# Value products of two attention units issued together, with six transposed blocks in flight

## The chip, the cores and the metric

One core of one Trainium2 chip runs the whole program. The metric is the device time of one execution in microseconds, as the median of several runs. The engines are named as the profile names them: PE is TensorE (PEld its weight loads), DVE is VectorE, ACT is ScalarE, POOL is GpSimd, and SP is SyncE, which here only issues DMAs.

## The reference, cut to what matters

One step of a hybrid layer: 2048 latent tokens on a 32 x 64 grid and 128 context tokens share one input projection of width 3840. Three branches read it: a gated short convolution, a chunked spatial gate and an attention over 8 heads of 64. The change touches the first and the last.

```
ya  = ba * conv3(ca * xa) * silu(ga)                # depthwise, over tokens, 256 channels
s   = q k_window * scale + bias[window], masked     # 8 x 16 window of the grid
s_c = q k_context * scale                           # 128 cached context keys
p   = softmax([s, s_c])
yc  = (p_window v_window + p_context v_context) * silu(gc)
out = concat(ya, yb, yc) @ w_out                    # then residual and LayerNorm
```

## The kernel before, in words

Each float32 operand is split into a high and a low float16 half, and a product is three matmuls (high x high, high x low, low x high). The order of instructions on every engine is the order in which the program emits them. The program keeps a planner's clock `now` in nanoseconds: each projection matmul of n columns advances it by n/2.4 (`tick`), and every event that is due is emitted there. `post(delay, f)` sets an event, `drain(tags)` emits events of a kind at once.

After the first stage (normalisation, spatial gate, values) the kernel runs projection jobs, each over five token tiles (four of 512, one of 128). Per pair of heads `hp` (0 to 3) they are q, k, gc and then some of xa, ca and the double job ba/ga (after hp 1 and hp 3). After each k job an `Attn` object posts 17 units of attention (16 blocks of 128 grid queries, and the context queries as unit 16), so that attention of `hp` runs inside the projections that follow it.

A unit `u` has two heads `h`. `scores(u, h)` issues four matmuls into the PSUM tile `s` and the sum with bias and maximum on DVE (L1041, into `pt`). Then, by `a_step` after it: `expo` (ACT, L1050), `norm` (DVE), `high` (ACT, L1057, the high half of the probabilities into `PH`), `low` (DVE, L1060, the low half, and then POOL's table of bias and mask for three half units later, L998 and L1002), and `turn` (a DMA transpose on SP, L1067, from `PH` into `ptr`). `a_val` after the second head's `turn`, `values` issues the value products into the PSUM tile `o` (L1086: 6 matmuls of 64 columns per chunk of 128 keys, 4 or 5 chunks, one chunk for unit 16), and DVE gates the result (L1094, L1101). Half units follow each other at half of `pace`.

The double job ba/ga has two projections a tile, here called P1(t) and P2(t), t = 0 to 4. The convolution of tile t, conv(t), is five POOL instructions (L1181, L1184) into the tile `cvt`. DVE multiplies P1 into it (L1194); ACT takes the tanh of P2 (L553), DVE makes the gate (L554) and the product ya(t) (L1199), and SP stores it (L1200). All projections share three PSUM buffers (`PJ = 3`), so P2(4) takes the buffer of P1(3), which L1194 of tile 3 frees.

Near the end of the last double job `open_out` loads `w_out` in eight blocks through three buffers (`wos`, L1139); `wo_split(k)` splits each on ACT (L1144) and DVE (L1145), and a block's load can be issued when the split three before it is done. `first_out` loads the first rows of the concatenated branches, and `out_split` splits them (L1127, L1128). Then the output projection runs (L1333).

Of the kernel before, what the change touches and what calls it, by code (L numbers as in the profile page):

```python
# [22 lines left out]
P = 128  # L23
D = 1024
KB = 8
LAT = 2048
# [65 lines left out]
    a_val=(5700.0, 7500.0, 6200.0, 5600.0),  # L92
    a_step=(700.0, 700.0, 2100.0, 2750.0, 3700.0),
    out_open=1000.0,
# [44 lines left out]
def hybrid_step(ctx: ExitStack, tc: tile.TileContext, x_prompt, x_sample, cache_k, cache_v, c, c_ctx,  # L139
# [56 lines left out]
    ones = cons.tile([P, P], F32, name="ones")  # L196
    G.memset(ones, 1.0)

# [50 lines left out]
    xg, xp = open_pool("xphase", side="right")  # L249
    mg, modp = open_pool("modp", side="left")  # L250
# [88 lines left out]
    wsp = tmpA.tile([P, 4, P], F32, name="wsp", tag="cvt", bufs=2)  # L339
# [358 lines left out]
    def load_cache():  # L698
# [3 lines left out]
        ck_sb = tmpA.tile([P, 512], F32, name="ck_sb", tag="cvt", bufs=2)  # L702
# [302 lines left out]
    class Attn:  # L1005
        def __init__(self, hp, pace):
            self.hp = hp
            self.ys = None
            self.ts = {}
            for u in range(17):  # L1010
                for h in range(2):
                    post(T['a_start'][hp] + (u + T['a_half'] * h) * pace, lambda u=u, h=h: self.scores(u, h), ("as", hp, u))

        def scores(self, u, h):
# [24 lines left out]
            pt = ap.tile([P, 608], F32, name="pt", bufs=3)  # L1039
# [24 lines left out]
            def turn():  # L1064
                drain(("av", self.hp, u - T['av_guard']))
                t = ap.tile([P, 10, P], F16, name="ptr", bufs=4)
                SP.dma_start_transpose(out=t[:, 0:2 * wp // P, :], in_=pb[:, 0:2 * wp])  # L1067
                self.ts[u, h] = t
                if h == 1:
                    post(T['a_val'][self.hp], lambda: self.values(u, [self.ts.pop((u, e)) for e in range(2)], wp // P, n), ("av", self.hp, u))  # L1070
# [4 lines left out]
        def values(self, u, t, nch, n):  # L1075
            hp = self.hp
            o = aps.tile([P, P], F32, name="o", tag="o")
            for ch in range(nch):
                if ch == 0:
                    vt, kk = (v_ctx if u < 16 else v_pr)[:, hp, :], P  # L1080
                else:
                    rb, j = UNITS[u]
                    vt, kk = VW[:, RB_ROW0[rb] // 4 + ch - 1, j, :], min(P, n - (ch - 1) * P)
                for i, (a, b) in enumerate(((0, 0), (0, 1), (1, 0))):
                    for h in range(2):
                        PE.matmul(out=o[64 * h:64 * h + 64, :], lhsT=vt[0:kk, a * P + 64 * h:a * P + 64 * h + 64],  # L1086
                                  rhs=t[h][0:kk, b * nch + ch, :], start=(ch == 0 and i == 0),
                                  stop=(ch == nch - 1 and i == 2))
            now[0] += nch * 3 * 80.0
            if u < 16:  # L1090
                rb, j = UNITS[u]
                if j == 0:
# [317 lines left out]
```

## Time and profile before

| | |
|---|---|
| median of 3 runs | 1134.43 us (1132.88 to 1136.36) |
| the profiled execution | 1134.04 us |
| its span, first to last instruction | 1132.3 us |
| PE busy | 1057.5 us, 93% |
| DVE, ACT, POOL busy | 70%, 40%, 31% |
| mean granted TensorE clock | 0.976 of full speed |

The span is that of the instructions on the core; 1.7 us of the execution's time lie around it. A busy engine is not the same as an engine at its best: matmuls overlap, so the distance from one matmul's start to the next one's is read in preference to its duration.

### The profile page before, as it was taken

To read this page: it belongs to the slowest core of one execution; us is meant where nothing else is said; L and a number is where in the kernel's file an instruction comes from. 1 tells how busy PE (TensorE), PEld (TensorE's weight loads), DVE (VectorE), ACT (ScalarE), POOL (GpSimd) and SP (SyncE) were. 2 spreads that over 40 slices of the span, in tenths; PEclk is the share of its full clock that TensorE was granted. 3 is DMA by queue.
4 is the path that set the end of the run, shared out by engine and by line. 5 is a ranking of instruction groups with operands and counts; after the bars stand their busy time and mean duration, and the time that the engine had idled before them with its cause. 6 is when DMAs were issued, how large, how long until landed. Compare 5 with 4: busy or idle time off the path is not lost. (4 is left out here: it accounts for less than half of the span.)

```text
span 1132.3 us, 21078 instructions
## 1 busy us (share of the span) xinstructions
PE 1057.5 (93%) x8044; PEld 680.0 (60%) x8044; DVE 791.7 (70%) x2072; ACT 449.5 (40%) x777; POOL 345.4 (31%) x428
## 2 busy tenths in 40 slices
PE   4588989988999999999998999999999999999996
PEld 1376875566784555555544545555455558888885
DVE  4676885775565367773677845886489866888887
ACT  1432332232232356553555634775377541121210
POOL 0144766300002023300374302430123632444442
PEclk8798999999999999999999999999999999999999
DMA  9813321438757347756456674685677667444441
GB/s 326 292 44 109 110 73 39 139 111 253 236 192 207 67 90 130 140 111 141 96 97 134 128 167 111 130 161 120 131 143 138 122 221 230 146 143 149 134 131 56
DMA packets 251605, 161.31 MB, mean 142 GB/s; under 512 B 162896, under 2 KB 224104, under 8 KB 251504
## 3 DMA queue, kind: packets, MB, share of 16 engines
q1 hardware_dynamic: 251504, 159.96, 54.8%
q8 instruction: 63, 1.03, 0.4%
q14 instruction: 38, 0.31, 0.1%
HBM read 85.96 MB, written 34.11 MB: 106 GB/s over the span
## 5 line engine op out<-in xcount | busy, mean ns | idle before, releaser
L537 PEld LDWEIGHTS <-wring 128*128 128x128 f16 x2400 | 211.4, 98 | 211.6 <-issue 2.9
L537 PE MATMUL pj<-h_hi,wring 128*128 128x512 f16 (+1 forms) x1280 | 335.8, 348 | 0.3 <-DVE scal L623 0.3
L537 PE MATMUL pj<-h_lo,wring 128*128 128x512 f16 (+1 forms) x640 | 217.4, 348 | 0.0
L1333 PE MATMUL ps<-wo,yh 128*128 128x512 f32 (+1 forms) x840 | 189.7, 388 | 0.0
L1333 PEld LDWEIGHTS ps<-wo,yh 128*128 128x128 f32 x840 | 155.0, 188 | 34.6
L1050 ACT ACTIVATE pt<-pt,sm,scal 128x608 f32<-128x608 f32 (+2 forms) x128 | 108.3, 846 | 71.2 <-DVE sm L1046 67.9
L1057 ACT ACTIVATE PH<-pt,sm 128x608 f16<-128x608 f32 (+3 forms) x136 | 99.8, 734 | 71.7 <-ACT pt L1050 53.2
L1060 DVE SCALAR_TENSOR_TENSOR PH<-pt,sm,PH 128x608 f16<-128x608 f32 (+3 forms) x136 | 111.0, 816 | 3.9 <-ACT PH L1057 3.7
L1041 DVE CUSTOM_DVE_ANT_0 pt<-s,TB 128x608 f32<-128x608 f32 (+2 forms) x128 | 93.4, 729 | 22.5 <-PE s L1029 15.9
L547 PE MATMUL vvps<-wV,h_hi 128*128 128x256 f16 x544 | 94.6, 278 | 8.4 <-DVE vt L920 8.4
L547 PEld LDWEIGHTS <-h_hi 128*128 128x128 f16 x816 | 81.7, 101 | 26.1 <-issue 13.8
L1002 POOL TENSOR_TENSOR TB<-raw,msk 128x480 f32<-128x480 f32 (+2 forms) x96 | 94.6, 989 | 0.1
L537 PE MATMUL p<-h_hi,wring 128*128 128x512 f16 (+1 forms) x320 | 84.8, 349 | 0.0
L998 POOL TENSOR_TENSOR tg<-PH 128x1 f32<-128x1 f16 x84 | 17.2, 205 | 216.1 <-DVE PH L1060 205.0
L537 PEld LDWEIGHTS <-wB 128*128 128x128 f16 x768 | 63.6, 99 | 24.3 <-DVE wB L241 0.4
L547 PE MATMUL vvps<-wV,h_lo 128*128 128x256 f16 x272 | 75.6, 278 | 0.0
L537 PE MATMUL ups<-h_hi,wB 128*128 128x128 f16 (+2 forms) x448 | 70.7, 267 | 0.3 <-DVE wB L241 0.3
L1362 ACT ACTIVATE r<-r,omv 128x1024 f32<-128x1024 f32 x15 | 18.7, 1247 | 124.7 <-issue 107.6
L1363 POOL TENSOR_TENSOR r<-r,gam 128x1024 f32<-128x1024 f32 x15 | 36.1, 2406 | 99.8 <-ACT r L1362 99.8
L1221 DVE SCALAR_TENSOR_TENSOR KL<-pj,scal,KH 64x512 f16<-64x512 f32 (+1 forms) x40 | 26.8, 670 | 54.0 <-ACT KH L1220 53.9
L499 POOL TENSOR_TENSOR h_lo<-hf,h_hi 128x512 f16<-128x512 f32 x34 | 40.0, 1180 | 76.2 <-DVE h_hi L496 50.4
L490 ACT ACTIVATE hf<-tp,modT 128x128 f32<-128x128 f32 (+2 forms) x64 | 33.6, 577 | 67.8 <-PE tp L478 50.1
(221 smaller groups left out, 1694.8 us busy)
## 6 DMA issues: line engine op xcount, KB each, us to landing
wa<-in_w_ada_dram SPq DMA_DIRECT2D x24, 512.0 KB
wraw<-in_w_in_dram SPq DMA_DIRECT2D x20, 512.0 KB
yf<-y_d SPq DMA_DIRECT2D x17, 512.0 KB
xt<-in_x_sample_dram SPq DMA_DIRECT2D x16, 512.0 KB
wj_d<-wsp SPq DMA_DIRECT2D x16, 512.0 KB
VW<-v_d SPq DMA_DIRECT2D x64, 128.0 KB
wring<-wj_d SPq DMA_DIRECT2D x16, 512.0 KB
xr<-in_x_sample_dram SPq DMA_DIRECT2D x16, 512.0 KB
```

What stands on the lines that cost most here:

```text
L490: S.activation(out=hf[:, a], in_=tp[:, a], func=AF.Identity, scale=modT[:, 8 + k, m:m + 1], bias=modT[:, k, m:m + 1])
L499: G.tensor_tensor(out=h_lo[:, k0:k0 + g, t0:t0 + n], in0=hv, in1=hi, op=ALU.subtract)
L537: PE.matmul(out=ps, lhsT=w(a, k) if callable(w) else w[:, a, k, :], rhs=mov(b, k), start=(k == 0 and i == 0), stop=(k == KB - 1 and i == 2))
L547: PE.matmul(out=ps, lhsT=a[:, k, i * P:(i + 1) * P], rhs=w[:, b, k, :], start=(k == 0 and q == 0), stop=(k == KB - 1 and q == 2))
L1002: G.tensor_tensor(out=TB[:, tslot(u) + h, P:P + n], in0=raws[h][:, off:off + n], in1=msk[:, mo:mo + n], op=ALU.add)
L1041: V.tensor_tensor_reduce(out=pt[:, :w], in0=src, in1=TB[:, tslot(u) + h, 0:w], op0=ALU.add, op1=ALU.max, scale=1.0, scalar=-3e38, accum_ou ...
L1050: S.activation(out=pt[:, :w], in_=src, func=AF.Exp, bias=sm[:, 1:2], scale=st_["isig"], accum_out=sm[:, 2:3])
L1057: S.activation(out=pb[:, 0:w], in_=pt[:, :w], func=AF.Copy, scale=sm[:, 3:4])
L1060: V.scalar_tensor_tensor(out=pb[:, wp:wp + w], in0=pt[:, :w], scalar=sm[:, 3:4], in1=pb[:, 0:w], op0=ALU.mult, op1=ALU.subtract)
L1221: V.scalar_tensor_tensor(out=KL[a, h, t0:t0 + n], in0=ps[a], scalar=ckk[a], in1=KH[a, h, t0:t0 + n], op0=ALU.mult, op1=ALU.subtract)
L1333: PE.matmul(out=ps, lhsT=yh[:, a, k, :], rhs=wo[:, b, k, f0:f1], start=(k == 0 and q == 0), stop=(k == KB - 1 and q == 2))
L1363: G.tensor_tensor(out=r, in0=r, in1=gam, op=ALU.mult)
```

## The change

Value products: `turn` no longer posts `values` for each unit. It collects two units (an even one and the odd one behind it; unit 16 alone), and one call issues the matmuls of both, unit after unit, into the two halves of one `o` tile, and then the two DVE gates. `turn` drains the value products of a finished pair only at the first head. Buffers: `ptr` goes from four to six blocks; in their place `pt` goes from three to two, `cvt` from two to one (its tag also holds `wsp` and `ck_sb` early in the kernel), and `ones` moves to a pool that is closed before the attention. Because `cvt` has one buffer, `conv(ti + 1)` is called at the end of a tile, behind ya and its store, and no longer behind P1. The planner's times `a_val` and `out_open` change.

```diff
-    a_val=(5700.0, 7500.0, 6200.0, 5600.0),
+    a_val=(5700.0, 6500.0, 5700.0, 5600.0),
-    out_open=1000.0,
+    out_open=2000.0,
...
-    ones = cons.tile([P, P], F32, name="ones")
-    G.memset(ones, 1.0)
...
     xg, xp = open_pool("xphase", side="right")
+    ones = xp.tile([P, P], F32, name="ones")
+    G.memset(ones, 1.0)
...
-    wsp = tmpA.tile([P, 4, P], F32, name="wsp", tag="cvt", bufs=2)
+    wsp = tmpA.tile([P, 4, P], F32, name="wsp", tag="cvt", bufs=1)
...
-            pt = ap.tile([P, 608], F32, name="pt", bufs=3)
+            pt = ap.tile([P, 608], F32, name="pt", bufs=2)
...
             def turn():
-                drain(("av", self.hp, u - T['av_guard']))
-                t = ap.tile([P, 10, P], F16, name="ptr", bufs=4)
+                if h == 0:
+                    drain(("av", self.hp, u - 3 if u % 2 == 0 else u - 2))
+                t = ap.tile([P, 10, P], F16, name="ptr", bufs=6)
                 SP.dma_start_transpose(out=t[:, 0:2 * wp // P, :], in_=pb[:, 0:2 * wp])
                 self.ts[u, h] = t
                 if h == 1:
-                    post(T['a_val'][self.hp], lambda: self.values(u, [self.ts.pop((u, e)) for e in range(2)], wp // P, n), ("av", self.hp, u))
+                    self.todo.append((u, [self.ts.pop((u, e)) for e in range(2)], wp // P, n))
+                    if u % 2 or u == 16:
+                        todo, self.todo = self.todo, []
+                        post(T['a_val'][self.hp], lambda: self.values(todo), ("av", self.hp, u))
...
-        def values(self, u, t, nch, n):
+        def values(self, todo):
             hp = self.hp
-            o = aps.tile([P, P], F32, name="o", tag="o")
+            o = aps.tile([P, 2, P], F32, name="o", tag="o")
+            for q, (u, t, nch, n) in enumerate(todo):
...
+                        for h in range(2):
+                            PE.matmul(out=o[64 * h:64 * h + 64, q, :], lhsT=vt[0:kk, a * P + 64 * h:a * P + 64 * h + 64],
+                                      rhs=t[h][0:kk, b * nch + ch, :], start=(ch == 0 and i == 0),
+                                      stop=(ch == nch - 1 and i == 2))
+                now[0] += nch * 3 * 80.0
+            for q, (u, t, nch, n) in enumerate(todo):
...
+                    V.scalar_tensor_tensor(out=self.ys[:, :, j * 16:j * 16 + 16], in0=o[:, q].rearrange("p (r c) -> p r c", c=16),
...
-                ct = tmpA.tile([P, 512], F32, name="cvt", bufs=2)
+                ct = tmpA.tile([P, 512], F32, name="cvt", bufs=1)
...
                 cvt = cvts.pop(ti)
-                conv(ti + 1)
                 V.scalar_tensor_tensor(out=cvt[:, :n], in0=p1[:, :n], scalar=wa_["c"], in1=cvt[:, :n], op0=ALU.mult, op1=ALU.mult)
...
                 SP.dma_start(out=y_d[idx, :, t0:t0 + n], in_=ya[:, :n])
+                conv(ti + 1)
                 if ti == 1:
                     job_load(cidx + 3)
```

## Rows read from the trace of the kernel before

**Rows 1.** The page's first part: the span, then each engine's busy time, share of the span and instructions.

```profile
span 1132.3 us, 21078 instructions
PE 1057.5 (93%) x8044; PEld 680.0 (60%) x8044; DVE 791.7 (70%) x2072; ACT 449.5 (40%) x777; POOL 345.4 (31%) x428
```

**Rows 2.** Busy time of each engine by stage: attention of hp 1 with the first double job, attention of hp 3 with the second one, and the output projection. Columns: stretch, its length, then PE, PEld, DVE, ACT and POOL busy with their instructions, granted clock, DMA share, GB/s.

```profile
515.00:670.00 155.00, 148.32 (x1193) 78.60 (x1191) 104.29 (x288) 74.00 (x136) 52.00 (x72) 0.99 0.62 128
...
800.00:932.00 132.00, 129.94 (x1110) 69.88 (x1109) 101.22 (x263) 74.52 (x128) 53.29 (x72) 1.00 0.67 149
932.00:1132.00 200.00, 189.79 (x845) 154.98 (x842) 159.85 (x333) 35.74 (x34) 79.91 (x33) 0.99 0.44 141
```

**Rows 3.** The chain that ended last, in order of time, the longest of its pieces: start, length, what.

```profile
932.24 189.57 PE ps L1333 x840
```

**Rows 4.** PE's instructions in order of time around the value products of one unit of 24 matmuls, and around those of unit 16, with 6. Columns: start, length, engine, line, operation, out<-in, count of those merged into the row.

```profile
413.82 0.38 PE L537 MATMUL pj<-h_lo,wring 128*128 128x512 f16 x1
414.13 0.36 PE L1086 MATMUL o<-ptr,v_ctx 128*64 128x128 f16 x6
414.32 0.67 PE L1086 MATMUL o<-ptr,VW 128*64 128x128 f16 x18
414.92 0.60 PE L537 MATMUL pj<-h_hi,wring 128*128 128x512 f16 x2
...
509.88 0.38 PE L537 MATMUL pj<-h_lo,wring 128*128 128x512 f16 x1
510.10 0.59 PE L537 MATMUL pj<-h_hi,wring 128*128 128x512 f16 x2
510.62 0.36 PE L1086 MATMUL o<-ptr,v_pr 128*64 128x128 f16 x6
510.91 0.39 PE L537 MATMUL pj<-h_lo,wring 128*128 128x512 f16 x1
```

**Rows 5.** The instructions that use the tile `o`, one group: DVE's gate of a unit, once a unit (min, median and longest duration in ns, first and last start).

```profile
L1094 DVE SCALAR_TENSOR_TENSOR yc<-o,scal,sgc x64: 330/343/352, 415.3 to 903.0; 128x128 f32<-128x128 f32 x64
```

**Rows 6.** Who waited for whom, in us in total, times, and the longest; the first four rows are PE's wait for transposed blocks in the stretches 375 to 515, 515 to 670, 670 to 800 and 800 to 932 (hp 0 to 3), the last two are of the stretch 515 to 670.

```profile
PE o L1086 <- DMA ptr<-PH: 0.5, 2, 0.4
...
PE o L1086 <- DMA ptr<-PH: 5.4, 3, 4.1
...
PE o L1086 <- DMA ptr<-PH: 1.5, 2, 1.0
...
PE o L1086 <- DMA ptr<-PH: 1.8, 3, 1.1
...
PE s L1026 <- DVE sm L1041: 0.9, 1, 0.9
...
DVE pt L1041 <- POOL TB L1002: 4.8, 5, 2.9
```

**Rows 7.** The longest of these waits (unit 7 of hp 1): SP's issues before it, PE's first value products after it, and the stretch right behind it (columns as in rows 2; the granted clock is the number before the DMA share).

```profile
601.87 0.32 SPq L1200 DMA_DIRECT2D y_d<-ya  x1
602.78 4.04 SPq L1067 DMA_TRANSPOSE ptr<-PH  x2
...
608.22 0.48 PE L1086 MATMUL o<-ptr,v_ctx 128*64 128x128 f16 x5 [4.13 <-DMA ptr<-PH]
...
607.90:611.40 3.50, 3.18 (x33) 2.09 (x33) 2.25 (x5) 1.68 (x3) 2.22 (x3) 0.51 0.67 150
```

**Rows 8.** The first instruction of conv(1) of the first double job on POOL, the table behind that convolution, and DVE's instruction that waited for that table.

```profile
572.76 1.22 POOL L1181 TENSOR_SCALAR cvt<-z,conv_sb 128x512 f32<-128x512 f32 x1
...
578.66 1.09 POOL L1002 TENSOR_TENSOR TB<-raw,msk 128x480 f32<-128x480 f32 x1
...
579.79 0.79 DVE L1041 CUSTOM_DVE_ANT_0 pt<-s,TB 128x608 f32<-128x608 f32 x1 [2.87 <-POOL TB L1002]
```

**Rows 9.** The second double job near its end, in order of time by engine: conv(2) on POOL, first and last instruction; conv(3), first, second and last; then on ACT the last block of `w_out`, the first half of `out_split` and the tanh of tile 2; then on DVE the split of the fourth block, ya(2) and the multiplication of P1(3) into `cvt`; and PE's change to the output projection.

```profile
900.21 0.69 POOL L1181 TENSOR_SCALAR cvt<-z,conv_sb 128x512 f32<-128x512 f32 x1 [3.43 <-DVE ya L1199]
...
903.82 1.27 POOL L1184 TENSOR_TENSOR cvt<-cvt,c 128x512 f32<-128x512 f32 x1
...
911.16 0.69 POOL L1181 TENSOR_SCALAR cvt<-z,conv_sb 128x512 f32<-128x512 f32 x1 [6.08 <-DVE ya L1199]
911.83 2.71 POOL L1181 TENSOR_SCALAR c<-z,conv_sb 128x512 f32<-128x512 f32 x1
...
917.61 2.20 POOL L1184 TENSOR_TENSOR cvt<-cvt,c 128x512 f32<-128x512 f32 x1
...
924.53 1.06 ACT L1144 ACTIVATE wo<-wos 128x1024 fp32r<-128x1024 f32 x1 [1.06 <-DMA wos<-in_w_out_dram]
...
926.32 1.06 ACT L1127 ACTIVATE yh<-yf 128x1024 fp32r<-128x1024 f32 x1 [0.73 <-DMA yf<-y_d]
927.28 0.67 ACT L553 ACTIVATE th<-p,scal 128x512 f32<-128x512 f32 x1
...
917.45 1.23 DVE L1145 TENSOR_TENSOR wo<-wos,wo 128x1024 fp32r<-128x1024 f32 x1 [1.83 <-ACT wo L1144]
...
929.27 0.75 DVE L1199 SCALAR_TENSOR_TENSOR ya<-th,scal,cvt 128x512 f32<-128x512 f32 x1
929.93 0.75 DVE L1194 SCALAR_TENSOR_TENSOR cvt<-p,scal,cvt 128x512 f32<-128x512 f32 x1
...
932.04 10.24 PE L1333 MATMUL ps<-wo,yh 128*128 128x512 f32 x44
```

More of the change, by code (lines that the diff above doesn't have):

```diff
@@ L701, in load_cache @@
         SP.dma_start(out=cv_sb, in_=cache_v[0, 0].rearrange("t h d -> t (h d)"))
-        ck_sb = tmpA.tile([P, 512], F32, name="ck_sb", tag="cvt", bufs=2)
+        ck_sb = tmpA.tile([P, 512], F32, name="ck_sb", tag="cvt", bufs=1)
         SP.dma_start(out=ck_sb, in_=cache_k[0, 0].rearrange("t h d -> t (h d)"))
@@ L1009, in __init__ @@
             self.ts = {}
+            self.todo = []
             for u in range(17):
@@ L1073, in scores @@
                 post(at, f, tg)
-        def values(self, u, t, nch, n):
+        def values(self, todo):
             hp = self.hp
-            o = aps.tile([P, P], F32, name="o", tag="o")
-            for ch in range(nch):
-                if ch == 0:
-                    vt, kk = (v_ctx if u < 16 else v_pr)[:, hp, :], P
-                else:
[L1082 to L1092, printed above, removed]
-                    self.ys = yst.tile([P, 8, 64], F32, name="yc", tag="yst")
-                V.scalar_tensor_tensor(out=self.ys[:, :, j * 16:j * 16 + 16], in0=o.rearrange("p (r c) -> p r c", c=16),
-                                       scalar=st_["cpv"], in1=sgc[:, u * P:(u + 1) * P].rearrange("p (r c) -> p r c", c=16),
-                                       op0=ALU.mult, op1=ALU.mult)
-                if j == 3:
-                    SP.dma_start(out=y_d[4 + hp, :, rb * 512:(rb + 1) * 512], in_=self.ys.rearrange("p r c -> p (r c)"))
-            else:
-                ys = yst.tile([P, P], F32, name="yp", tag="yst")
-                V.scalar_tensor_tensor(out=ys, in0=o, scalar=st_["cpv"], in1=sgc[:, LAT:TOK], op0=ALU.mult, op1=ALU.mult)
-                SP.dma_start(out=y_d[4 + hp, :, LAT:TOK], in_=ys)
@@ new lines, in values @@
+            o = aps.tile([P, 2, P], F32, name="o", tag="o")
+            for q, (u, t, nch, n) in enumerate(todo):
+                for ch in range(nch):
+                    if ch == 0:
+                        vt, kk = (v_ctx if u < 16 else v_pr)[:, hp, :], P
+                    else:
+                        rb, j = UNITS[u]
+                        vt, kk = VW[:, RB_ROW0[rb] // 4 + ch - 1, j, :], min(P, n - (ch - 1) * P)
+                    for i, (a, b) in enumerate(((0, 0), (0, 1), (1, 0))):
+                        for h in range(2):
[3 more added lines that the diff above has]
+                now[0] += nch * 3 * 80.0
```

11 lines of the change are left out of this document (added).

## The prediction

> **What bounds the kernel now.** I read the page's first part: PE is busy for 1057.5 of 1132.3 us, no other engine for more than 791.7 [rows 1]. Then the stages, where the reader is to see that in both attention stretches with a double job PE is idle for only 6.7 of 155 and 2.1 of 132 us [rows 2]. Then the chain that ended last: its last long piece is 189.57 us of output projection, which begins the moment the last job's matmuls end [rows 3]. So the kernel is PE from front to back. What PE spends less on is won if nothing stops it later; what stops it is lost in full. Then PE in order of time around the value products [rows 4], PE's waits by stretch [rows 6], and the queues of DVE, ACT and POOL where the convolution was moved [rows 8, 9].
>
> **Value products.** A burst of value products costs more than its matmuls. With 24, the last projection matmul in front starts at 413.82 and the first behind at 414.92: 1.10 us. With 6, the second of two that begin at 510.10 starts one step later, at 510.32 (the step of 512 columns is 510.10 - 509.88 = 0.22), and the one behind at 510.91: 0.59. So 18 matmuls are 0.51 us, 0.028 each, and a burst has a fixed 1.10 - 24 x 0.028 = 0.43, of which 0.215 is the projection step itself. About 0.22 us is paid for going in and out of the 64-column shape [rows 4]. There are 64 grid units and 4 of unit 16, 68 bursts [rows 5]; pairs leave 32 + 4. 32 x 0.22 = **7.0 us won**. The lower bound is 0 (if the second unit in a pair pays again), the upper 32 x 0.43 = 14. I take 7.0, since between chunks of one burst, which also change weights and blocks, the rows show no such gap.
>
> The Trainium skill (TensorEngine Tiling (Array Packing), section Tiling Modes, key properties) says the same: a change of tiling mode, not of tile, drains the engine. An estimate from the constant of 166 ns in TensorE: Matmul & The Clock Gate (section Single matmul latency), twice a burst, would be 10.6 us. The trace's 0.22 a burst is smaller and decides.
>
> **Waits of PE for transposed blocks.** They are 0.5 + 5.4 + 1.5 + 1.8 = 9.2 us; in hp 1 come 0.9 for DVE [rows 6]. Behind the longest, 4.13 us, the granted clock is 0.51 for 3.5 us, the lower of its two levels (1.2 of 2.4 GHz), which costs another 1.7 [rows 7]. With pairs the even unit's blocks have a whole `pace` more, and the odd unit's matmuls start after the even unit's, 0.7 to 0.8 us into the burst; against that `a_val` is 1.0 (hp 1) and 0.5 (hp 2) shorter. In hp 0 and 2 there are two waits each [rows 6], single late transfers, 2.0 us in all: I take 1.7 won. In hp 3 DVE is busy for 101 of 132 us [rows 2] and I take the waits for its lateness, against which the burst's 0.8 helps once: 0.8 won of 1.8.
>
> In hp 1 the order on POOL matters. conv(1) runs from 572.76 to the table at 578.66, and DVE waits 2.87 us for that table, in all 4.8 in this stretch [rows 6, 8]; with DVE late, ya(1) is late, its store holds SP's queue until 601.87, and the transposes behind it go out at 602.78: that is the 4.13 us wait [rows 7]. In the new order conv(1) stands behind ya(0), so the table of 578.66 can go some 4 us earlier and the lateness does not build up there. But conv(1), conv(2) and conv(3) then each block tables for some 5 us further on, where DVE waits 2 to 3 us each. I leave 2 us of PE waits in hp 1, without the drop of the clock: 5.4 + 0.9 + 1.7 - 2 = 6.0 won. Bounds: 0 (as many waits as before) to 8.0. Together **8.5 us won** (2.5 to 10.5).
>
> **Buffers.** `pt` with two: the reuse two half units later stands on DVE's own queue behind its last reader L1060, so nothing new is waited for. `ptr` with six: the slot a pair asks for belongs to a pair planned 1.4 to 3.3 us earlier than the transpose, as before. The two gates behind a pair are the same work on DVE. `ones`, `wsp`, `ck_sb`: the second user of the `cvt` slot is loaded long after the first is read. I take 0 for all; if `pt` did wait, it would be on DVE in hp 3, and the price the hp 3 wait of 1.8 once more.
>
> **The single `cvt`.** conv(t+1) now waits for ya(t). After P2(t) that takes tanh, gate and ya (2.2 us if the queues are clear), a convolution (900.21 to 905.09, 4.9; or 911.16 to 919.81, 8.65, beside DVE's splits) and L1194 (0.75) [rows 9]: 8 us. PE needs the result when P2(t+2) starts, P1(t+1), P2(t+1) and P1(t+2) later. For full tiles that is 15.4 us. At the end P1(4) has 128 columns, and it is 5.2 + 5.2 + 1.3 = 11.7.
>
> There the queues are not clear. The output projection starts at 932.04, P2(4) 1.3 earlier (24 steps of a quarter of 0.215), at 930.7, and L1194 of tile 3 ends at 930.68: no slack now. ya(2) starts at 929.27 only, because ACT's tanh of tile 2 stands behind the split of the last `w_out` block (until 925.59) and `out_split` (926.32) [rows 9]. Before, that did no harm, since conv(3) waited for ya(1) and began at 911.16.
>
> By the planner: the four jobs after k of hp 3 take 4 x 21.76 = 87.04 us, scores 14.93, values 17.52, together 119.49. `open_out` is due 96.40 (before) or 97.40 in, 23.09 or 22.09 before the end; P2(2) ends 12.80 before it. Rounded up to matmuls, `out_split` falls 13.65 before the end, ahead of the tanh; with the new `out_open` 12.59, behind ya(2) and conv(3). But the eight splits stay ahead, and three in place of four of them stand ahead of L1194 of tile 2. That one now waits for conv(2), which starts where conv(3) did (911.16) and ends near 918.9; the fourth split moves from 917.45 to 919.7, and the loads that it frees are 2.3 later. So: last split on ACT ends near 927.0, tanh 927.8, ya(2) 928.9 to 929.7, conv(3) (5.4, part beside `out_split`) to 935.1, L1194 to 935.9. PE waits from 930.7: **5.2 us lost**. A wait of this length was followed by the low clock [rows 7], so **1.7 more**: 6.9. Bounds: conv 4.9 and loads not later, 3.3 without the clock; conv 8.65, 8.4 and 1.7, 10.1. All of the tail after it hangs on PE and moves with it.
>
> **Sum.** -7.0 - 8.5 + 6.9 = -8.6. Against the profiled execution's own time, 1134.04 (the span of 1132.3 and 1.7 around it; the median is 0.4 above): **1125.4 us**.
>
> **Rivals.**
> - *No stall at the end.* ACT comes to the tanh at once, conv(3) is done before 930. For it: PE has 11.7 us where a clear chain needs 8. Against: the splits on ACT wait for loads until 924.53 [rows 9]. 1134.04 - 15.5 = 1118.5.
> - *hp 1 wins nothing.* The moved convolutions block tables as often, DVE (104 us busy of 155 on average [rows 2], nearly full in the double job) stays late. 1134.04 - 7.0 - 2.5 + 6.9 = 1131.4.
> - *Slower: the single `cvt` makes each tile's convolution PE's bound.* Place: L1194 in both double jobs. The second instruction of conv(3) took 2.71 us against 0.69 of the first, beside DVE's splits [rows 9]; with conv at 8.65 the end costs 10.1, and in hp 1 PE waits a further 4.1 + 1.7, as in rows 7, while nothing is won there: 1134.04 - 9.5 + 10.1 + 5.8 = 1140.4. It decides from 9.5 us of loss on.
> - *No saving from pairs*, the second unit paying again: 1134.04 - 8.5 + 6.9 = 1132.4.
>
> The Trainium skill (SBUF — State Buffer, section Who interferes with whom) has the rule behind the slower rival: the port pair of DVE and GpSimd is an exclusive lock, and the second to come blocks fully. The 2.71 us agrees.
>
> **How the numbers follow.** Forecast 0.48, no stall at the end 0.17, hp 1 wins nothing 0.18, slower 0.10, no saving 0.07. A measurement of this kernel tells about 0.3%, 3.4 us, from no change: faster means below 1131.0, slower above 1137.8. Faster: 0.45 of the forecast, 0.17, and 0.08 of the third, 0.70; same 0.19; slower 0.11 (the fourth and a little). The range 1118 to 1133 holds the forecast, half of the first rival, the third and the fifth, 0.8; the forecast's own is 1120 to 1130.
>
> **What would show it.** After: 36 bursts, each 0.22 over its matmuls; fewer waits for `ptr` in hp 0 to 2; conv(1) on POOL behind ya(0), DVE's longest wait for TB under 2.9; POOL's conv(3) behind ya(2), then a wait of DVE for it, and 3 to 8 us of idle PE before the last 24 matmuls of L537, with a low clock behind. The prediction is wrong if that gap is missing, if the longest hp 1 wait stays, or if a second L1086 unit in a pair begins with a gap.

## The result, and the profile after

The changed kernel takes 1151.84 us (median; 1149.59 to 1152.77) against 1135.39 of the kernel before on the same chip: 1.0134 times as long, 95% interval 1.0105 to 1.0163. It is 1.3% slower, and the prediction said 0.8% faster. In the changed kernel the names are P1 x `cvt` L1199 (L1194 before), gate L553, ya L1204, tanh L552, splits of `w_out` L1150/L1151, value products L1091, output projection L1339.

The page's first part and the windows of [rows 2], then two short windows at the end of the last double job, and last the stretch from k of hp 3 to the output projection, after and before. Columns as in [rows 1, 2].

```profile
span 1149.2 us, 21089 instructions
PE 1059.9 (92%) x8044; PEld 685.7 (60%) x8044; DVE 785.7 (68%) x2072; ACT 448.9 (39%) x777; POOL 341.1 (30%) x428
...
515.00:670.00 155.00, 148.46 (x1205) 79.21 (x1204) 102.10 (x288) 76.31 (x140) 51.78 (x72) 1.00 0.65 132
800.00:932.00 132.00, 126.11 (x1062) 67.12 (x1060) 92.08 (x255) 70.28 (x125) 42.65 (x62) 1.00 0.62 134
935.90:942.80 6.90, 2.72 (x24) 2.56 (x24) 3.80 (x4) 2.32 (x3) 2.38 (x3) 0.51 0.20 64
946.20:949.60 3.40, 3.40 (x27) 3.21 (x25) 1.11 (x2) 0.95 (x2) 1.90 (x5) 0.50 0.20 77
...
787.40:948.40 161.00, 145.28 (x1177) 78.49 (x1174) 104.91 (x278) 78.25 (x136) 48.10 (x70) 0.97 0.63 137
...
786.70:932.00 145.30, 143.24 (x1175) 76.02 (x1173) 108.06 (x279) 78.70 (x136) 53.29 (x72) 1.00 0.69 151
```

Most of the loss is PE idle in hp 3: from k to the output projection it grows from 145.30 - 143.24 = 2.1 to 161.00 - 145.28 = 15.7 us. At its end stand two stretches at the granted clock of 0.5, its lower level. PE's waits, from 400 us to the output projection (line waited for: total, times, longest), answer [rows 6]:

```profile
PE s L1026 <- DVE sm L1041: 7.2, 14, 1.3
PE o L1091 <- DMA ptr<-PH: 6.9, 10, 2.5
PE p L536 <- DVE th L553: 6.1, 1, 6.1
PE p L536 <- DVE cvt L1199: 3.8, 1, 3.8
PE s L1034 <- DVE sm L1041: 3.3, 4, 2.2
```

The waits for transposed blocks fell from 9.2 to 6.9, and the longest from 4.13 to 2.5. In their place stand 10.5 us for score buffers (0.9 before) and 9.9 us in two waits at the end (none before). A burst, PE in order of time, against [rows 4]:

```profile
432.60 0.38 PE L536 MATMUL pj<-h_lo,wring 128*128 128x512 f16 x1
432.91 0.36 PE L1091 MATMUL o<-ptr,v_ctx 128*64 128x128 f16 x6
433.10 0.67 PE L1091 MATMUL o<-ptr,VW 128*64 128x128 f16 x18
433.61 0.34 PE L1091 MATMUL o<-ptr,v_ctx 128*64 128x128 f16 x6
433.78 0.67 PE L1091 MATMUL o<-ptr,VW 128*64 128x128 f16 x18
434.38 0.39 PE L536 MATMUL pj<-h_hi,wring 128*128 128x512 f16 x1
```

48 matmuls take 434.38 - 432.60 = 1.78 us, and 1.78 - 48 x 0.028 = 0.44, against 0.43 before: a pair pays the fixed part once, as costed.

The end, against [rows 9]: SP's queue (SPq: start and length of an issue), before and then after; then ACT, POOL, DVE, and PE's two waits in brackets, all after.

```profile
906.34 0.32 SPq L1102 DMA_DIRECT2D y_d<-yp  x1
906.90 1.28 SPq L1139 DMA_DIRECT2D wos<-in_w_out_dram  x3
911.09 0.33 SPq L1200 DMA_DIRECT2D y_d<-ya  x1
...
910.62 0.32 SPq L1108 DMA_DIRECT2D y_d<-yp  x1
914.87 0.32 SPq L1205 DMA_DIRECT2D y_d<-ya  x1
915.41 1.30 SPq L1145 DMA_DIRECT2D wos<-in_w_out_dram  x3
...
919.62 2.00 ACT L1150 ACTIVATE wo<-wos 128x1024 fp32r<-128x1024 f32 x2 [6.29 <-DMA wos<-in_w_out_dram]
934.81 1.06 ACT L1150 ACTIVATE wo<-wos 128x1024 fp32r<-128x1024 f32 x1 [2.10 <-DMA wos<-in_w_out_dram]
936.54 1.06 ACT L1133 ACTIVATE yh<-yf 128x1024 fp32r<-128x1024 f32 x1 [0.68 <-DMA yf<-y_d]
937.50 0.67 ACT L552 ACTIVATE th<-p,scal 128x512 f32<-128x512 f32 x1
...
940.34 0.69 POOL L1187 TENSOR_SCALAR cvt<-z,conv_sb 128x512 f32<-128x512 f32 x1 [20.56 <-DVE ya L1204]
943.91 1.26 POOL L1190 TENSOR_TENSOR cvt<-cvt,c 128x512 f32<-128x512 f32 x1
...
939.49 0.75 DVE L1204 SCALAR_TENSOR_TENSOR ya<-th,scal,cvt 128x512 f32<-128x512 f32 x1
945.21 0.75 DVE L1199 SCALAR_TENSOR_TENSOR cvt<-p,scal,cvt 128x512 f32<-128x512 f32 x1 [4.97 <-POOL cvt L1190]
...
939.51 0.27 PE L536 MATMUL p<-h_hi,wring 128*128 128x128 f16 x1 [6.05 <-DVE th L553]
946.01 0.21 PE L536 MATMUL p<-h_hi,wring 128*128 128x128 f16 x1 [3.79 <-DVE cvt L1199]
```

The first `w_out` loads stand behind ya(1)'s store, which waits on SP until 914.87; before, they were ahead of it, at 906.90. Of the 8.5 us between 906.90 and 915.41 the place behind that store accounts for half: the loads go out 4.79 us behind unit 16's store (910.62), 0.56 before. The other 4.3 us are that unit 16's store itself is late. The last split on ACT is 10.3 us later than before (924.53), the tanh of tile 2 stands behind it and behind `out_split`, and P1(4) waits for the gate. Then conv(3) can only start behind ya(2), and P2(4) waits for its result. The windows above show the clock in and behind both waits.

**By stages.** The lengths are taken from the first matmul of one job to the first of another, for the stretches that hold the attention of hp 0 (xa, ca, q), hp 1 (k up to and with the next k), hp 2 (gc, xa, q) and hp 3 (k to the output projection). The ratio is to the kernel before on the same chip. The last column counts the half units, of 33 in each hp, whose `low` stands on DVE behind the `norm` of the next half unit ("turned"). The time up to the first of these stages lay between 415 and 421 us in the profiled executions (410 in e11), whatever the kernel, so small differences are read from the stages. But a stage is that of one execution, and executions scatter: the kernel before lay between 1130.33 and 1142.31 us in 20 of them, and hp 2 of the changed kernel and of e1, the same code there, took 104.4 and 106.4. The stages of e2 are 7.7 us longer than those before, its ratio says 3.5 (1.1 to 6.0); those of e16 are 3.3 longer, its ratio says 2.4 shorter. Where the two disagree the ratio decides, and a difference of 2 us in one stage shows nothing.

```
kernel                           ratio [95%]             hp 0   hp 1   hp 2   hp 3  turned
before                           1                       95.2  173.1   99.7  145.3  0 5 0 1
after                            1.0134 [1.0105,1.0163]  94.0  170.4  104.4  160.9  3 3 4 4
e1  after, out_open 1000         1.0123 [1.0089,1.0158]  93.9  170.4  106.4  158.6  3 3 4 4
e2  before, out_open 2000        1.0031 [1.0010,1.0053]  95.1  173.4   99.7  152.8  0 5 0 1
e3  after, steps by due time     1.0076 [1.0045,1.0107]  93.3  172.2  101.6  157.8  0 4 0 1
e4  after, no pairs              1.0052 [1.0036,1.0067]  94.7  170.0  100.1  156.0  0 0 0 1
e5  before, one cvt              1.0062 [1.0038,1.0087]  95.0  174.4   99.8  152.4  0 5 0 1
e6  before, steps by due time    0.9957 [0.9938,0.9977]  95.3  168.6  100.4  149.9  0 1 0 1
e7  e3 + e1                      1.0037 [1.0021,1.0054]  93.3  172.3  101.6  154.2  0 4 0 1
e8  before, a_val of after       0.9974 [0.9955,0.9993]  95.1  169.6  100.1  145.4  0 0 0 1
e9  after, two cvt, open 1000    1.0046 [1.0028,1.0065]  93.9  170.1  106.4  151.5  3 3 4 4
e10 after, later values          1.0215 [1.0191,1.0238]  93.9  174.3  109.2  165.1  3 3 7 11
e11 e9 + e10                     1.0175 [1.0152,1.0198]  93.9  174.2  107.1  157.3  3 3 7 11
e12 e6 + e8                      0.9987 [0.9967,1.0006]  95.0  170.2  100.8  147.1  0 0 0 1
e13 e9, low at 2300              1.0329 [1.0303,1.0355] 117.2  185.6  101.2  149.1  2 1 0 2
e14 e13 + e3                     1.0510 [1.0485,1.0536] 126.1  199.3  101.8  147.6  0 0 0 0
e15 before, low at 2300          1.0291 [1.0264,1.0318] 114.2  188.3   99.8  145.9  0 0 0 0
e16 e9, low at 2300 in hp 2, 3   0.9979 [0.9962,0.9995]  93.9  170.1  101.2  151.3  3 3 0 2
e17 e16, out_open 0              0.9983 [0.9969,0.9997]  93.9  170.1  101.1  149.6  3 3 0 2
```

The change lost 15.6 us in hp 3 (its double job alone is 16.6 longer: 69.1 us for 52.5) and 4.7 in hp 2, and won 1.2 in hp 0 and 2.7 in hp 1.

### The profile page after: what moved, and what is told of

The parts are those of the page before. It is cut to its first block, busy times and chain, and to the rows that moved or that the text cites. A ratio compares the mean times of both kernels' runs of the same rounds, so it can differ in the third digit from the quotient of the medians.

```text
span 1149.2 us, 21089 instructions
## 1 busy us (share of the span) xinstructions
PE 1059.9 (92%) x8044; PEld 685.7 (60%) x8044; DVE 785.7 (68%) x2072; ACT 448.9 (39%) x777; POOL 341.1 (30%) x428
## 5 line engine op out<-in xcount | busy, mean ns | idle before, releaser
L536 PEld LDWEIGHTS <-wring 128*128 128x128 f16 x2400 | 216.9, 99 | 228.3 <-issue 15.0
L1339 PE MATMUL ps<-wo,yh 128*128 128x512 f32 (+1 forms) x840 | 190.3, 389 | 0.0
L1339 PEld LDWEIGHTS ps<-wo,yh 128*128 128x128 f32 x840 | 155.6, 189 | 34.6
L1060 DVE SCALAR_TENSOR_TENSOR PH<-pt,sm,PH 128x608 f16<-128x608 f32 (+3 forms) x136 | 106.4, 783 | 4.4 <-ACT PH L1057 4.1
```

The source lines that it names most:

```text
L536: PE.matmul(out=ps, lhsT=w(a, k) if callable(w) else w[:, a, k, :], rhs=mov(b, k), start=(k == 0 and i == 0), stop=(k == KB - 1 and i == 2))
L1060: V.scalar_tensor_tensor(out=pb[:, wp:wp + w], in0=pt[:, :w], scalar=sm[:, 3:4], in1=pb[:, 0:w], op0=ALU.mult, op1=ALU.subtract)
L1339: PE.matmul(out=ps, lhsT=yh[:, a, k, :], rhs=wo[:, b, k, f0:f1], start=(k == 0 and q == 0), stop=(k == KB - 1 and q == 2))
```

## The experiments

Theories for the end: A, the late `w_out` loads; B, the single `cvt`. For hp 2 and 3: C, the planner's clock jumps by a pair's value products at once and turns DVE's order round; D, `pt` with two buffers.

**e1 and e2: `out_open` alone.**

```diff
-    out_open=2000.0,      # e1, in the changed kernel; e2 is the reverse edit in the kernel before
+    out_open=1000.0,
```

> The changed kernel with out_open back at 1000. Theory A (SP's order): with 2000 open_out comes behind P2(1), so the eight loads of w_out stand behind ya(1)'s store on SP and begin at 915.4 in place of 906.9, and every split and the tanh of tile 2 are some 9 us late. With 1000 the loads go first again: first w_out load within 1 us of the store of unit 16's result, PE's two waits in the last tiles (6.05 and 3.79 us) become one of 3 to 6, the time falls by 5 to 9 us, to 1143 to 1147. Theory B (the single cvt alone makes the end late, the loads do not matter): within 2 us of 1151.8, the waits stay near 10 us in sum.

> The kernel before with out_open at 2000, nothing else. Theory A (SP's order): the loads of w_out fall behind ya(1)'s store, the tanh of tile 2 comes 6 to 9 us later than 927.3, P1(4) and P2(4) wait for their PSUM buffers: 5 to 9 us slower than before, 1140 to 1144. Theory B (only with the single cvt does the end hang on ACT): within 2 us of before, since conv(3) starts behind ya(1) here.

In the kernel before, the 1000 ns put the loads behind ya(1)'s store, 5.3 us behind unit 16's, and lengthened the last double job by 8 us in the profiled execution; by the ratio e2 is 3.5 us slower. SP and PE in e2, then SP in e1:

```profile
902.81 0.32 SPq L1102 DMA_DIRECT2D y_d<-yp  x1
...
907.56 0.32 SPq L1200 DMA_DIRECT2D y_d<-ya  x1
908.11 1.30 SPq L1139 DMA_DIRECT2D wos<-in_w_out_dram  x3
...
931.19 0.26 PE L537 MATMUL p<-h_hi,wring 128*128 128x128 f16 x1 [5.17 <-DVE th L554]
...
911.27 0.32 SPq L1108 DMA_DIRECT2D y_d<-yp  x1
911.82 1.28 SPq L1145 DMA_DIRECT2D wos<-in_w_out_dram  x3
```

That is A, in the kernel before by itself. Taking it back in the changed kernel won only 2.3 us in hp 3, and 2.2 of the median where 5 to 9 were expected: the loads were ahead of the store again, but at 911.82, and the two waits of PE were still 3.7 and 4.2 us. So A is a cause, but not one that adds to the other.

**e3 and e4: due times; no pairs.** In e3 the steps of a half unit are dated from the time at which its scores were due, not from the time at which they were issued. In e4 values go out unit by unit, all else as changed.

```diff
+    at = T['a_start'][hp] + (u + T['a_half'] * h) * pace          # e3
+    post(at, lambda u=u, h=h, due=now[0] + at: self.scores(u, h, due), ("as", hp, u))
...
+            back = min(0.0, due - now[0])
...
-                post(at, f, tg)
+                post(at + back, f, tg)
-                    drain(("av", self.hp, u - 3 if u % 2 == 0 else u - 2))      # e4
+                    drain(("av", self.hp, u - 3))
...
-                    if u % 2 or u == 16:
-                        todo, self.todo = self.todo, []
-                        post(T['a_val'][self.hp], lambda: self.values(todo), ("av", self.hp, u))
+                    todo, self.todo = self.todo, []
+                    post(T['a_val'][self.hp], lambda: self.values(todo), ("av", self.hp, u))
```

> The changed kernel, with the five steps of a half unit (expo to turn) dated from the time at which its scores were due and not from the moment at which they were issued. Theory C (the planner's clock jumps 2.4 us at a pair, scores behind it are issued late and their steps with them, so that norm of the next half unit overtakes low of the one before on DVE and DVE waits for ACT's exp): PE's waits for s, 10.5 us in the changed kernel, fall below 4, DVE's waits of L1053 fall in hp 2 and hp 3 from 10.3 and 7.8 to about 5, the time falls by 4 to 7 us, to 1145 to 1148. Theory D (pt with two buffers is what holds the scores): no change, 1150 to 1154.

> The changed kernel with value products unit by unit again; buffers, convolution, a_val and out_open stay as changed. Theory C (the pair's jump): the waits for s fall below 4 us of 10.5, and the 32 bursts that come back cost 7 us, so the time is within 3 us of 1151.8. Theory D (pt with two buffers): the waits for s stay and 7 us come on top, 1157 to 1160. The end (PE's last two waits) stays as in the changed kernel for both.

PE's waits in e4, from 415 us on, all that there are:

```profile
PE o L1090 <- DMA ptr<-PH: 8.0, 13, 1.1
PE p L536 <- DVE cvt L1198: 5.9, 1, 5.9
PE p L536 <- DVE th L553: 3.8, 1, 3.8
```

Without pairs no wait for a score buffer is left, though `pt` has two: D falls, and the pairs, meant to save 7 us, cost 9.1 us of median. With due times the turned half units of hp 2 go from 4 to 0 and hp 2 from 104.4 to 101.6; the time falls by 6.6 us by the ratios, as expected, but the waits for score buffers only from 10.5 to 6.7, not below 4. This is what "turned" looks like, DVE in hp 2, first after and then before:

```profile
743.15 0.77 DVE L1041 CUSTOM_DVE_ANT_0 pt<-s,TB 128x608 f32<-128x608 f32 x1
...
745.23 0.15 DVE L1053 TENSOR_SCALAR sm<-sm 128x1 f32<-128x1 f32 x1 [1.05 <-ACT pt L1050]
...
745.50 0.83 DVE L1060 SCALAR_TENSOR_TENSOR PH<-pt,sm,PH 128x608 f16<-128x608 f32 x1
```

```profile
743.30 0.77 DVE L1041 CUSTOM_DVE_ANT_0 pt<-s,TB 128x608 f32<-128x608 f32 x1
...
744.30 0.85 DVE L1060 SCALAR_TENSOR_TENSOR PH<-pt,sm,PH 128x608 f16<-128x608 f32 x1
...
745.76 0.15 DVE L1053 TENSOR_SCALAR sm<-sm 128x1 f32<-128x1 f32 x1 [0.60 <-ACT pt L1050]
```

In order, `low` (L1060) fills the time in which ACT makes the next half unit's exponentials, and `norm` (L1053) then waits 0.60. Turned, DVE waits 1.05 first and does `low` afterwards, and the sum that frees the score buffer for PE is late. In all of hp 2 DVE waits 10.3 us for the exponentials (before: 5.7).

**e5, e9: the single `cvt` alone, and taken back.** e5 is the kernel before with one `cvt` and `conv(ti + 1)` moved as in the change. e9 is the changed kernel with two; the room comes from the scratch tile of the convolution, which shares the buffer of the tanh. The diff shows its main lines; two small tiles also move from `c2` to `cvt`, and `wsp` and `ck_sb` have two buffers again.

```diff
-                ct = tmpA.tile([P, 512], F32, name="cvt", bufs=1)        # e9, with out_open=1000.0
+                ct = tmpA.tile([P, 512], F32, name="cvt", bufs=2)
-                    o = ct if q == 0 else tmpA.tile([P, 512], F32, name="c2")
+                    o = ct if q == 0 else tmpA.tile([P, 512], F32, name="c2", tag="th")
...
                 cvt = cvts.pop(ti)
+                conv(ti + 1)
...
-                conv(ti + 1)
```

> The kernel before with one change alone: one buffer for cvt, and conv(t+1) called behind ya(t); out_open stays at 1000, values go unit by unit. Theory B (the single cvt alone makes PE wait, as the prediction costed it for the end): a wait of 3 to 8 us ahead of the last projection P2(4), the low clock behind it, the end of the program some 5 to 9 us longer, time 1.0 to 1.01 of before even if the first double job wins up to 3 us. Rival B2 (the single cvt costs only together with the late w_out loads of out_open 2000): no wait over 1 us at the end, the end within 2 us of before, and the time 0 to 3 us shorter. The stretch of hp 1 tells what its gain of 2.7 us in the changed kernel came from: about -3 us here if it is the moved conv(1), 0 if it is ptr or a_val.

> The changed kernel with two buffers for cvt again, conv(t+1) back behind P1(t) and out_open 1000; the room comes from the convolution's scratch tile c2, which shares the buffer of the tanh. Theory B: the end of the program (P1(0) of the last double job to the output projection, 69.1 us in the changed kernel, 52.4 before) falls back to 51 to 54, without a wait of PE over 1 us, and the time by 13 to 17, to 1135 to 1139: level with before, since the waits for scores (5.1 us in hp 2, 2.8 in hp 3) eat what the pairs save. Rival B3: the pairs themselves lengthen the end (33.1 us from P1(0) to P2(1) in the changed kernel, 29.0 without pairs), and it stays above 57.

PE's two waits at the end of e5:

```profile
929.44 0.22 PE L537 MATMUL p<-h_hi,wring 128*128 128x128 f16 x1 [1.09 <-DVE th L554]
935.95 0.26 PE L537 MATMUL p<-h_hi,wring 128*128 128x128 f16 x1 [5.01 <-DVE cvt L1193]
```

B is right: hp 3 is 7.1 us longer. hp 1 gets 1.3 longer, not shorter, so the gain there didn't come from the moved convolution. In e9 the two long waits at the end are gone, but hp 3 stays 6.2 us over before. That is B3 in part: with pairs hp 3 has its own waits (3.6 us for score buffers, 2.6 for transposed blocks, 1.7 for the gate of tile 3), and its loads start at 909.97. The 1.7 belong to e9's own edit and not to the pairs: because the scratch tile shares the buffer of the tanh, ACT holds the tanh of tile 3 until POOL's last convolution is done.

```profile
936.33 0.69 ACT L552 ACTIVATE th<-p,scal 128x512 f32<-128x512 f32 x1 [4.47 <-POOL cvt L1190]
```

Set side by side, hp 3 is longer than before by 7.5 us with the late loads alone (e2), 7.1 with the single `cvt` alone (e5), 6.2 with pairs and two `cvt` (e9), 10.6 with the single `cvt` and the late loads (e4), 13.3 with the single `cvt` and pairs (e1), and 15.6 with all three. The single `cvt` and the pairs add up; the late loads cost only 2.3 to 3.6 beside the single `cvt`.

**e6, e7, e8, e12: due times and `a_val`.** e6 is e3's edit in the kernel before, e7 is e3 and e1 together, e8 the kernel before with `a_val` of the changed one, e12 is e6 and e8 together.

> The kernel before with the steps of a half unit dated from the planner's due time of its scores and not from the moment they were issued. Theory C (a late clock of the planner, as pairs make it, is what turns DVE's order round): the kernel before advances its clock by one unit's value products at a time and has few turned steps, so 1130 to 1137, no change, with the five turned steps of hp 1 gone. If dating from the issue cost something in the kernel before as well, 1 to 3 us are won in hp 1. Rival: steps that are dated earlier than their scores' issue put DVE on work whose input is not there, and it is slower by 2 us or more.

> The changed kernel with both repairs, steps dated from the due time and out_open 1000. If the two causes are independent, their gains add: 1151.8 - 8.7 - 2.2 = 1141, and the end still holds two waits of PE of 3 to 5 us each for the single cvt. If the due times also bring ya(2) and its convolution forward, the end falls below 60 us (52.4 in the kernel before) and the time to 1136 or less. If it stays at 1143, out_open costs nothing beside the single cvt.

> The kernel before with the a_val of the changed one alone (6500 for 7500 in hp 1, 5700 for 6200 in hp 2). Theory: the shorter delay takes no time from PE by itself and leaves the transposes less time, so PE waits for ptr a little more: 1134 to 1140. Rival: hp 1's gain of 3 us in the changed kernel comes from it (value products earlier, DVE's queue shifted): 1130 to 1133.

> The kernel before with steps dated from the due time and the a_val of the changed kernel together. Each alone took 3.5 to 4.5 us from hp 1. If both work by keeping DVE's order through conv(1), they don't add: 1130 to 1133. If they add: 1126 to 1129. Steps by due time also lengthened the end by 5 us with a wait of 2.6 us for the gate; if that comes from due times in general it shows again (end 57), and if it was an accident of when the tanh fell among the w_out splits, the end is 53.

Both e6 and e8 take the turned half units out of hp 1 (5 to 1, 5 to 0) and 4.5 and 3.5 us of its length. e8's expectation was wrong: `a_val` alone gives the kernel before what the changed one gained in hp 1, so that gain most likely comes from it; the changed kernel with the old `a_val`, or six `ptr` blocks alone, was not run. They don't add in e12, where hp 1 is 170.2; its time, 1135.67, is level with before, where 1130 to 1133 was expected if they don't add. e7 came out better than the sum of the two: 1138.92 us against 1141. e6 lengthened hp 3 by 4.5 us with one wait of 2.6 us for a gate and the clock's fall; e12 has that wait with 1.3 us and no fall, and I did not find what decides. The profiled execution of e6 took 1134.50 us, 3.8 above its median of 1130.74, so most executions may not have that fall.

**e10, e11: where the burst falls.** Only `a_val` moves; e11 has e9's buffers too.

```diff
-    a_val=(5700.0, 6500.0, 5700.0, 5600.0),
+    a_val=(5700.0, 5900.0, 6450.0, 6050.0),
```

> The changed kernel with a_val alone changed, to 5900, 6450 and 6050 in hp 1 to 3. A pair's value products are planned 3.7 us + a_val behind the scores of its last half unit, and scores come every 3.0, 3.0, 2.45 and 2.35 us (hp 0 to 3): in the changed kernel that is 0.13, 0.40, 0.84 and 0.96 of a half pace behind a score, so 2.6, 1.8, 0.4 and 0.1 us ahead of the next one, and PE's waits for score buffers are 0, 2.0, 5.1 and 3.5 us. Theory C2 (a burst of 1.8 us that falls due just ahead of the next scores makes them late and pushes them against the ones behind): with 2.4, 2.1 and 2.0 us ahead of the next scores these waits fall from 10.5 to under 3 us, hp 2 from 104.4 to 99 to 100 us, and the time by 5 to 9, to 1143 to 1147; the end stays near 69. Rival C3 (bursts of two are too long for two score buffers wherever they fall): the waits stay within 2 us of 10.5 and the time within 3 of 1152.

> Both of the runs before in one kernel: two buffers for cvt with out_open 1000, and the value products of a pair just behind the scores. If the two causes are all that is wrong, the pairs' 7 us show: 1126 to 1131, faster than before. If the end or the waits for scores stay, it is level with before, 1133 to 1139.

C2 fell, and the run turned it round: the waits for score buffers rose from 10.5 to 17.6 us. In the changed kernel bursts already stood directly behind scores (a value step is dated from the issue of its transpose, so it falls later than its plan). Scores move the planner's clock by 400 to 507 ns and a pair by 1920 or 2400, together by up to 2907. Half a pace is 3000 ns in hp 0 and 1, but 2450 in hp 2 and 2350 in hp 3: there a pair of 60 matmuls makes the next scores 457 and 557 ns late even when it stands directly behind scores, and later when it begins later. By the plan `low` comes 2750 behind its scores and the next `norm` half a pace + 700: the room between them is 950 ns in hp 0 and 1, but 400 in hp 2 and 300 in hp 3. The trace of the changed kernel bears this out: in hp 3 the four turned half units are the first heads of units 8, 10, 12 and 14, the four whose scores stand right behind a burst of 60, and in hp 2 three of these are turned; behind bursts of 48 none is. With `a_val` later, the turned ones went from 4 to 7 and from 4 to 11. (In hp 1 the shorter delay also cost waits for transposed blocks: 8.3 us, 4.5 in the changed kernel.) e11 shows the same: 1154.63 us, where 1126 to 1131 was hoped for.

**e13 to e17: the low step alone.** `low` is planned at 2300 in all hp, in e9 (e13), in e9 with due times (e14) and in the kernel before (e15); then in hp 2 and hp 3 alone, in e9 (e16), and with `out_open` 0 (e17).

```diff
-    a_step=(700.0, 700.0, 2100.0, 2750.0, 3700.0),
+    a_step=(700.0, 700.0, 2100.0, 2300.0, 3700.0),      # e13, e14, e15
...
-            for f, at in zip((expo, norm, high, low, turn), T['a_step']):                # e16, e17
+            steps = T['a_step'][:3] + ((2750.0, 2750.0, 2300.0, 2300.0)[self.hp],) + T['a_step'][4:]
+            for f, at in zip((expo, norm, high, low, turn), steps):
```

> The changed kernel with two cvt buffers (as in the run with two cvt and out_open 1000, 1141.0 us) and the low step planned 2300 instead of 2750 ns behind the scores. By the plan, norm of the next half unit falls half a pace + 700 behind the scores: 3700, 3700, 3150 and 3050 ns in hp 0 to 3. So low stands ahead of it as long as the next scores aren't more early against it than 950, 950, 400, 300 ns; with 2300 that is 1400, 1400, 850 and 750. Theory C (the order of low and norm on DVE is the cause): the turned pairs fall from 14 to under 5, PE's waits for score buffers from 9.6 to under 5 us, hp 2 from 106.4 to 100 to 102 us, and the time to 1132 to 1137. Rival C3 (bursts of two are too long for DVE whatever the order): the order is repaired, and the waits and hp 2 stay within 1.5 us.

> As the run before it, with steps dated from the due time too. Theory C: no turned pair is left, waits for score buffers under 4 us, and with the 6 us that the pairs save on PE the time is 1127 to 1133, under the kernel before. Rival C3: 1134 to 1139, level with it.

> The kernel before with the low step at 2300 alone. It has five turned pairs in hp 1, one in hp 3. Theory C: they go, hp 1 falls from 173.1 to 169 to 171 us, the time to 1130 to 1133. Rival (the order goes along with hp 1's waits but doesn't cause them): hp 1 stays at 172 to 174 and the time at 1134 to 1137.

In hp 2 it went as C said: 106.4 to 101.2 us in e13, with the turned ones down from 4 to 0. In hp 3 they fell from 4 to 2, and 151.5 to 149.1; e16, with the same step there, has 151.3, so in hp 3 no gain is shown. But hp 0 and hp 1 lost 23 and 15 us, and 19 and 15 in the kernel before (e15). DVE in hp 0 of e13, and its waits there:

```profile
440.81 0.15 DVE L1053 TENSOR_SCALAR sm<-sm 128x1 f32<-128x1 f32 x1 [0.54 <-ACT pt L1050]
...
442.09 0.85 DVE L1060 SCALAR_TENSOR_TENSOR PH<-pt,sm,PH 128x608 f16<-128x608 f32 x1 [0.92 <-ACT PH L1057]
442.86 0.78 DVE L1041 CUSTOM_DVE_ANT_0 pt<-s,TB 128x608 f32<-128x608 f32 x1
...
444.95 0.15 DVE L1053 TENSOR_SCALAR sm<-sm 128x1 f32<-128x1 f32 x1 [1.05 <-ACT pt L1050]
...
DVE sm L1053 <- ACT pt L1050: 22.9, 27, 1.1
DVE PH L1060 <- ACT PH L1057: 17.0, 25, 0.9
```

Now `low` stands ahead of the next sum (28 of 33 times in hp 0, once in the kernel before): DVE waits for ACT's `high`, the sum is late, the next exponentials are late, and DVE waits for those too. From one `norm` to the next it is 4.1 us here and 3.8 on average in hp 0, where half a pace is 3.0. So `low` has one place, behind the next sum and ahead of the next norm. My expectation saw the one side only. The steps are dated from the planner's clock behind the scores' own 400 to 507 ns, so in hp 0 and 1 a `low` at 2750 comes 150 to 257 ns behind the next scores, and at 2300 it comes 193 to 300 ahead of them; in hp 2 and 3, where half a pace is shorter, it stays behind them at either value. With due times, which date the steps as if no scores were issued late, the traces agree: `low` is ahead of the next sum 33 of 33 times in hp 0 and in hp 1 at 2300 (e14), once in each at 2750 (e3).

> The changed kernel with two cvt buffers and out_open 1000, and the low step at 2300 in hp 2 and hp 3 only. Theory C (low belongs between the next half unit's sum and its norm): 93.9 us in hp 0 and 170 in hp 1 as in the run with two cvt buffers, 101 in hp 2 and 90.6 in hp 3 as in the run with the early step, the end 58 to 59; so 1141.0 - 5.2 - 1.6 - 0.8 = 1133, between 1131 and 1136, level with the kernel before: the pairs' 6 us are there, and 2 us of waits for score buffers in hp 2 and some 4 us of waits at the end are against them. If hp 0 or hp 1 is longer all the same, the account by stages is wrong.

> The kernel of the run before with out_open at 0, so that the loads and splits of w_out come 1 us earlier by the plan. If the end's remaining waits (for the tanh behind the splits) hang on the loads, the end falls from 58.5 to 55 to 57 us and the time by 1 to 3. If not, no change.

e16 came out at 1133.26 us, as worked out, 0.2% under the kernel before (interval 0.9962 to 0.9995) and by the ratios 1.5% under the changed one. By stages hp 2 is where the gain was expected, and hp 3 isn't: 151.3 where 149 was worked out, so that the sum fits is in part luck. e17 is no different in the median within the measurement; its end is 1.7 us shorter in the trace, 59.0 us where 55 to 57 was expected. Against before, hp 0 and hp 1 of e16 are 1.3 and 3.0 us shorter, hp 2 is 1.5 longer (3.2 us of waits for score buffers are left), and hp 3 6.0, with 8.5 us of waits against 2.1; 1.7 of these are again the wait for the gate of tile 3 that e9's buffer brings.

## Why the prediction was wrong, step by step

- **Where the miss lies.** -8.6 us was forecast, and by the ratio +15.2 came (11.9 to 18.5). Without pairs the changed kernel is at +5.9 (4.1 to 7.6, e4). So the pairs cost some 9 us where 7.0 were to be won, which is 16 of the 24 us of the miss; all else cost 6 where 1.6 were to be won. The step that weighs most is thus the one from PE's own time to the kernel's: "What PE spends less on is won if nothing stops it later", with 0 put for what could stop it.
- **Value products, -7.0: right on PE itself.** Stages, less PE's idle time and half of the stretches at the lower clock in which it worked: before 513.2 - 10.8 - 1.6 = 500.8, e16 516.5 - 17.3 - 3.4 = 495.8, and 0.9 less in the jobs ahead of them; 5.9 us won on PE itself. The changed kernel won 500.8 - 497.2 + 0.9 = 4.5 there. All of it and more was given back as waits.
- **Waits for `ptr`, -8.5: too large, and for a wrong reason.** All four stages together fell by 2.3. In hp 1 6.0 of waits and clock was forecast; 5.4 + 0.9 + 1.7 = 8.0 stood there, and 4.5 for transposed blocks with 2.0 for score buffers stand after, 1.5 less. The step that conv(1) behind ya(0) keeps the lateness from building up is refuted by e5 (174.4 us, longest wait still 3.8). What helped was, by e8, `a_val`, which the prediction had put on the other side.
- **The single `cvt`, +5.2 and +1.7: right alone, wrong in the whole.** e5 has the wait at the place named, 5.01 us, and hp 3 is 7.1 us longer (6.9 forecast). The closeness is in part luck, since the 6.9 were counted with the late `out_open`, which e5 doesn't have. The step that the convolution is slow only beside DVE's splits held too: conv(3) took 945.17 - 940.34 = 4.83 us with DVE waiting, and 8.65 beside them [rows 9]. The Trainium skill's rule (SBUF — State Buffer, section Who interferes with whom), that the port pair which DVE and GpSimd share is an exclusive lock, agrees with these two numbers.
- **The step that failed at the end: "the eight splits stay ahead", with the last one near 927.0.** It followed `out_split` by the planner's clock, but not the queue past which the loads moved: `out_open` fell from one side of ya(1)'s store on SP to the other, by 1.0 us of plan, and the loads came 8.5 us later, about half of it for that store. The last split ended at 935.87, `out_split` (936.54) stood ahead of the tanh of tile 2 (937.50) and not behind it as counted, and a wait of 6.05 us ahead of P1(4) was added. The price of this by itself is 3.5 us by the ratio (e2; 7.5 in hp 3 of its profile), and 2.3 of hp 3 beside the rest (e1).
- **The step that was left out: what a burst of two does to the planner's clock.** "I take 0 for all" covered buffers and gates; nothing asked what is dated from an issue that a pair makes late. The 10.5 us of waits for score buffers come from the pairs (none in e4). The order of `low` and `norm` explains the larger part of hp 2's 4.7 us, of which 1.9 are left when it is put right by due times (e3) and 1.5 when it is put right by `low` (e16), but only some 4 of the 10.5: in both runs 6.7 us of these waits are left. What the pairs cost beyond that order is not traced to one step. A wait for `pt`, which the prediction feared, is not there.
- **The rivals.** The slower one had the right sign and, at the end, the right tile, but it took the moved convolution in hp 1 and DVE's port for the cause; neither showed, and 1140.4 was 9 us short of the 1149 to 1153 measured.
- **The signs.** Those that the prediction named came true: 36 bursts that pay once, conv(3) behind ya(2), 3.79 us of idle PE ahead of the last 24 matmuls with the lower clock behind, the longest wait in hp 1 down from 4.13 to 2.53. They tested the terms that held, and hardly those that failed.

Not run: a planner that charges what the rows show. It puts 40 ns on a value matmul and 2400 on a pair of 60; at 60 x 0.028 + 0.22 = 1.9 us a pair directly behind scores would stay within half a pace of hp 2.

Left open: why four half units stay turned in hp 1 under due times (e3, e7), how the 6 us that hp 3 of e9 and e16 is still longer divide, beyond the 1.7 of e9's buffer, and what makes the 2.2 us wait ahead of unit 16's scores in hp 2, which stands in e3 and e16 as in the changed kernel and not before.

## What to carry to other kernels

When a step is moved, walk it past every queue that it uses: 1 us of plan put eight loads behind a store that was waiting and made them 4 to 5 us late. Where the order of instructions comes from planned times, list the gaps between steps that must not pass each other (here 300 to 950 ns) and compare them with the lateness that the largest jump of the planner's clock leaves (2400 ns for a pair, 1200 before; 457 and 557 ns late in hp 2 and 3). And a step between two neighbours has a bound on both sides: moving `low` by 450 ns won 5 us in hp 2 and cost 23 in hp 0.

## What was not expected of the hardware

Two engines that hand work to each other (sum, exponentials, norm, high, low on DVE and ACT) lost a fifth of their pace from one exchange in DVE's order: 3.8 us for a half unit of hp 0 on average in e13, up to 4.1, in place of 3.1 before, with the sum and `low` as long as before (0.73 and 0.79 us). And the lower clock came behind shorter waits of PE than the 4.13 us of [rows 7]: in e8 3.4 us of it followed a wait of 1.64 us in hp 1, in the changed kernel one of 2.22 us in hp 2, while one of 2.53 us in hp 1 of the same execution was followed by none.
